# Another choice and order of seven-product pairs in the second feed-forward matrix of layer 1

## The chip, the cores and the metric

One NeuronCore of one Trainium2 chip runs the whole program. The times are device microseconds (us) of a run. In the profile PE is the matrix engine (PEld its weight loads), DVE the vector engine, ACT the scalar engine, POOL the general-purpose engine, and SP the queue that issues the loads from HBM. PSUM is the memory that matrix products accumulate in; it has eight banks here, each of 128 x 512 floats. SBUF is the memory that holds everything else.

## The reference

A two-layer decoder trunk for 256 tokens of width 2048, in float32. Layer 0 mixes tokens by retention, layer 1 by a short gated convolution; a SwiGLU feed-forward of width 5632 follows each, and a final RMSNorm closes the trunk. The change touches only the feed-forward of layer 1:

```
def swiglu(h, w_in, w_out):
    a, b = jnp.split(h @ w_in, 2, axis=-1)
    return (jax.nn.silu(a) * b) @ w_out
...
x = (x + g2 * swiglu(h, ffn_w_in[i], ffn_w_out[i])).astype(x.dtype)
```

`w_in` has 2048 x 11264 elements, `w_out` 5632 x 2048.

## The kernel before

**Products in three matmuls.** A float32 operand is written as hi + lo, two numbers that the matrix engine takes (`fp32r`). A product is then hi·hi + hi·lo + lo·hi, three matmuls (`triple`, lines 1190 to 1194: L1192, L1193, L1194). The weights come from HBM as float32, in loads of 128 x 2048 that `fetch` issues on SP (L388), three buffers in turn. `prepare` cuts a load into pieces of up to 1024 columns; for each, ACT makes hi (L426) and DVE makes lo = raw - hi (L429). There are four buffers for hi and four for lo, and `take` keeps up to three pieces ready.

**Pairs, plain and in sevens.** In layer 1's feed-forward (`swiglu_tokens`, `token_products`) the tokens are the rows of the result: two halves of 128 tokens by two column blocks of 512, which makes four results in four PSUM banks. The sum runs over *pairs* of 128-row weight tiles. One pair and four results are a 2 x 2 by 2 x 2 block product. A plain pair takes 8 block products, or 24 matmuls. A pair "in sevens" takes 7, or 21 matmuls, by a Strassen-Winograd scheme: three of them use blocks as they are, four use sums of blocks on both sides. Three of the seven go to the four result banks, four to four further banks:

```
plan = [
    ("m1", a11), (x_banks[1][0], s4), (x_banks[0][0], a12), ("m5", s1), ("m7", s3), ("m6", s2),
    (x_banks[0][1], a22),
]
```

The sums of the weight blocks are made for every load by DVE (L412, L417, L418); such a load is prepared in four pieces, of 512, 1024, 1024 and 1024 columns, and not in two of 1024. The sums of the other operand are made once per pair by `seven_sums` (L636 to L648): four DVE operations on 128 x 128 (L641 to L644), one ACT cast (L646), one DVE subtraction (L647). For pairs of the middle (silu(a) * b) they start from a float32 copy of the pair, made by ACT from PSUM (L1289) into a tile `full` that has one buffer. After the last pair in sevens of a group, ACT and DVE combine the four further banks (L1242 to L1246).

**Groups.** Each call of `token_products` is a group. I number them by matrix, part and place. The middle has 44 tiles, in two parts of 20 and 24 (`PART_TILES`):

- part 0: a first group in another form makes tiles 0 to 3, then *in 0.1* to *in 0.4* make 4 tiles (2 pairs) each; *out 0.0* and *out 0.1* multiply all 10 pairs with the second matrix, each for 1024 output columns.
- part 1: *in 1.0* to *in 1.5* make 12 pairs; *out 1.0* multiplies them for the first 1024 columns; the last 1024 columns are done in another form, with no sevens.

Every *in* group goes over 8 pairs of the input, with pairs 2, 4 and 6 in sevens: plain, plain, seven, plain, seven, plain, seven, plain. The *out* groups take their order from `ffn_token_groups` (L165 to L201). With the pairs of a part numbered from 0 and those in sevens in brackets, it is now 0 1 5 6 [2] 7 [3] [4] 8 9 in part 0 and 8 9 3 4 [0] 5 [1] 6 [2] 7 10 11 in part 1.

**Seams.** The tail of a group runs within the next one. `token_products` hands back "asides", which `ticked` starts after so many blocks of the next group's products. After an *in* group (`middle`, L1269) these are: the finals, silu and product for each token half during the next group's first pair, and, at the end of its second pair, `turned`: eight transposes on PE (L1264) into two PSUM banks, from which ACT and DVE make hi and lo of the new middle tiles (L1285, L1286) and, for a pair that will be taken in sevens, ACT makes `full`. After an *out* group (`outputs`, L1294) they are 16 transposes in two portions, and updates of the residual (L1303).

The eight PSUM banks are two lanes of four (L1187, L1203). A group's results use one lane, which changes from group to group; the further banks of its sevens use the other, and so do the transposes of the group before. The first pair in sevens of a group therefore takes its banks m1, m5, m7, m6 from those that the transposes have left.

**What sets the order.** PE's order is that of the program text (L290). DVE's and ACT's order in this stage is chosen by a planner from its own model of costs. SP issues loads in the order of use, each when one of the three `raw` buffers is free. The weights lie in HBM in the order of use (`in_use_order`, `laid_out`), so a new order of pairs makes another layout, and the same number of loads.

Of the kernel before, what the change touches and what calls it, by code (L numbers as in the profile page):

```python
# [50 lines left out]
TOKEN_LAYERS = (1,)  # L51
PART_TILES = (20, 24)
IN_SEVENS = {0: (), 1: (2, 4, 6)}
OUT_SEVENS = {0: 3, 1: 3}
RAW_BUFS = 3
PART_BUFS = 4
ROW_AT = 64
# [65 lines left out]
def led(cols):  # L123
    return [Group(cols[:LEAD])] + [Group([c]) for c in cols[LEAD:]]
# [35 lines left out]
def token_group(cols, pairs, sevens):  # L160

    return [Group.sevens(cols, p) if p in sevens else Group(cols, DV, p) for p in pairs]


def ffn_token_groups(layer):  # L165

    n = KT // 2
    rows = [(2 * i, 2 * i + 1) for i in range(n)]
    tiles = DV // P
    ins, outs, at = [], [], 0  # L170
    for part, size in enumerate(PART_TILES):
        groups = []
        for j in range(at // tiles, (at + size) // tiles):
            if j == 0:
                narrow = [q * DFF + i * P for i in range(tiles) for q in range(2)]
                groups += led(narrow)
            else:
                groups.append(token_group([j * DV, DFF + j * DV], rows, [rows[i] for i in IN_SEVENS[layer]]))
        ins.append(groups)
        pairs = [(at + 2 * i, at + 2 * i + 1) for i in range(size // 2)]  # L180
        fixed = pairs[:2] if part == 0 else pairs[-4:-2]
        late = pairs[-2:]
        rest = [p for p in pairs if p not in fixed + late]
        sevens = rest[: OUT_SEVENS[layer]]
        plain = rest[OUT_SEVENS[layer] :]
        mixed = fixed + plain[:2]
        plain = plain[2:]
        for p in sevens:
            mixed += [p] + plain[:1]
            plain = plain[1:]  # L190
        mixed += plain + late
        assert sorted(mixed) == pairs
        outs.append([])
        for half in range(2):
            c = half * 2 * DV
            if layer == DEPTH - 1 and part == 1 and half == 1:
                outs[-1].append([Group([c + i * P], ks=range(at, at + size)) for i in range(2 * tiles)])
            else:
                outs[-1].append(token_group([c, c + DV], mixed, sevens))
        at += size  # L200
    return ins, outs  # L201
# [7 lines left out]
FFN_IN = ffn_in_groups()  # L209
FFN_OUT = out_groups(halves(DFF), 2, LEAD_FFN)  # L210
FFN_TOKENS = {layer: ffn_token_groups(layer) for layer in TOKEN_LAYERS}


# [1217 lines left out]
```

## Time and profile before

| | us |
|---|---|
| runs | 2618.07, 2621.07, 2623.72; median 2621.07 |
| the profiled execution, as timed | 2622.86 |
| its span, first to last instruction | 2620.8 |
| PE busy | 2577.0 (98% of the span) |
| DVE busy | 2166.4 (83%) |
| ACT busy | 1296.0 (49%) |

In the views of the profile, a line such as L429 is a line of the kernel; `lo<-raw,hi` says which tile an operation writes and which it reads. Two rows of one engine overlap in time when the next instruction starts before the end of the last is over, so that distances between starts tell more of the rate than the lengths do. "Idle before" is how long the engine stood still, and the name behind the arrow is what ended that. A view of stretches gives, for each stretch of time, its length, the busy time of each engine and the clock that PE was granted, as a share of the full one.

### The profile page before, as it was taken

Reading aid. Unit: us, or ns where it says so; the run is one execution under the profiler, and the core shown is the slowest. Engines: PE = TensorE matmul, PEld = TensorE weight load, DVE = VectorE, ACT = ScalarE, POOL = GpSimd, SP = SyncE. Lnnn points to the kernel's source line nnn. Section 1 sums busy time; section 2 is a strip of 40 time slices with the busy share of each in tenths; the row PEclk is TensorE's granted clock in tenths of the full one; section 3 lists DMA queues with packets and bytes.
Section 4 is the critical chain, followed back from the end, with each engine's and each line's share of the span. In section 5 each row is a group of like instructions: output and inputs, shape, how many; then the busy total and the mean of one; then the engine's idle time right before and its main releaser. Section 6 shows DMA issues by size and latency. Waiting matters only on the chain.

```text
span 2620.8 us, 36671 instructions
## 1 busy us (share of the span) xinstructions
PE 2577.0 (98%) x14350; PEld 2244.8 (86%) x14350; DVE 2166.4 (83%) x2726; ACT 1296.0 (49%) x1747; POOL 128.5 (5%) x230
## 2 busy tenths in 40 slices
PE   6999999999999999999999999999999999999998
PEld 5998889888889888888888898888987888788887
DVE  7898878787698887777778889888888987898974
ACT  5544543444455544344444454444565544555553
POOL 0000000120000001100000100000000000000000
PEclk9999999999999999999999999999999999999999
DMA  9976668777686987878787768877755555455553
GB/s 399 395 276 239 230 229 319 275 291 275 242 303 238 339 321 292 299 297 300 289 302 286 299 230 327 322 289 284 262 187 183 193 205 181 177 193 203 200 192 129
DMA packets 96944, 687.48 MB, mean 262 GB/s; under 512 B 10753, under 2 KB 12545, under 8 KB 13825
## 3 DMA queue, kind: packets, MB, share of 16 engines
q1 hardware_dynamic: 96194, 684.48, 70.4%
q8 instruction: 112, 1.84, 0.3%
q10 hardware_dynamic: 576, 0.66, 0.1%
q14 instruction: 62, 0.51, 0.1%
HBM read 682.99 MB, written 2.10 MB: 261 GB/s over the span
## 4 chain that ended last, share of the span: by engine, by line
PE 67%; issue 28%; DVE 2%; DMA 1%; ACT 0%; POOL 0%; SPq 0%; POOLq 0%; ACTq 0%; DVEq 0%
PE bank L480 30%; PE bank L483 15%; PE bank L518 4%; PE bank L519 4%; PE bank L520 4%; PE bank L505 1%; PE bank L504 1%; PE bank L503 1%; PE bank L548 1%; PE bank L547 1%; PE bank L546 1%; PE bank L693 1%; PE bank L694 1%; PE bank L695 1%; DMA raw<-w_all 1%
## 5 line engine op out<-in xcount | busy, mean ns | idle before, releaser
L426 ACT CAST hi<-raw 128x1024 fp32r<-128x1024 f32 (+1 forms) x912 | 934.6, 1033 | 939.0 <-PE bank L480 357.0
L429 DVE TENSOR_TENSOR lo<-raw,hi 128x1024 fp32r<-128x1024 f32 (+1 forms) x912 | 1084.1, 1198 | 303.9 <-ACT hi L426 301.1
L480 PE MATMUL bank<-h,hi 128*128 128x512 f32 x2016 | 699.8, 392 | 0.0
L483 PE MATMUL bank<-h,lo 128*128 128x256 f32 x2016 | 565.6, 281 | 0.0
L480 PEld LDWEIGHTS bank<-h,hi 128*128 128x128 f32 x2016 | 377.8, 187 | 81.7
L483 PEld LDWEIGHTS bank<-h,lo 128*128 128x128 f32 x2016 | 381.8, 189 | 0.0
L332 DVE SCALAR_TENSOR_TENSOR raw<-raw,cb 128x2048 f32<-128x2048 f32 x160 | 365.6, 2285 | 17.2 <-DMA raw<-w_mod 17.1
L480 PE MATMUL bank<-mid,hi 128*128 128x512 f32 x922 | 320.1, 394 | 0.0
L483 PE MATMUL bank<-mid,lo 128*128 128x256 f32 x922 | 256.5, 278 | 0.4 <-DVE lo L429 0.4
L480 PEld LDWEIGHTS bank<-mid,hi 128*128 128x128 f32 x922 | 173.2, 188 | 39.5
L518 PE MATMUL bank<-hi,h 128*128 128x512 f32 x512 | 201.7, 394 | 0.0
L519 PE MATMUL bank<-lo,h 128*128 128x512 f32 x512 | 200.8, 392 | 0.0
L520 PE MATMUL bank<-hi,h 128*128 128x512 f32 x512 | 199.8, 390 | 0.0
L1192 PE MATMUL bank<-hi,h 128*128 128x512 f32 x490 | 193.3, 394 | 0.0
L1193 PE MATMUL bank<-lo,h 128*128 128x512 f32 x490 | 192.3, 392 | 0.0
L1194 PE MATMUL bank<-hi,h 128*128 128x512 f32 x490 | 192.1, 392 | 0.0
L483 PEld LDWEIGHTS bank<-mid,lo 128*128 128x128 f32 x922 | 173.4, 188 | 0.7 <-DVE lo L429 0.7
L480 PE MATMUL bank<-rm,hi 128*128 128x512 f32 x496 | 173.0, 395 | 0.0
L429 DVE TENSOR_TENSOR lo<-sums,hi 128x1024 fp32r<-128x1024 f32 x78 | 95.4, 1223 | 60.6 <-ACT hi L426 60.1
L426 ACT CAST hi<-sums 128x1024 fp32r<-128x1024 f32 x78 | 82.1, 1053 | 126.2 <-PE bank L1194 92.6
L483 PE MATMUL bank<-rm,lo 128*128 128x256 f32 x496 | 138.0, 278 | 0.0
L520 PEld LDWEIGHTS bank<-hi,h 128*128 128x128 f32 x512 | 96.6, 189 | 20.6
(230 smaller groups left out, 4095.6 us busy)
## 6 DMA issues: line engine op xcount, KB each, us to landing
raw<-w_all SPq DMA_DIRECT2D x456, 1024.0 KB, 4.9
raw<-w_mod SPq DMA_DIRECT2D x192, 1024.0 KB, 5.3
x<-x_in SPq DMA_DIRECT2D x4, 512.0 KB, 5.5
decay<-tab_in SPq DMA_DIRECT2D x8, 128.0 KB, 3.1
out<-x SPq DMA_DIRECT2D x4, 256.0 KB, 3.2
out<-x ACTq DMA_DIRECT2D x3, 128.0 KB, 2.6
out<-x SPq DMA_DIRECT2D x1, 384.0 KB, 2.6
out<-x ACTq DMA_DIRECT2D x1, 256.0 KB, 3.2
```

The costliest lines, as they stand in the source:

```text
L332: nc.vector.scalar_tensor_tensor(raw, raw, 1.0, cb, op0=ALU.mult, op1=ALU.mult, accum_out=total)
L426: nc.scalar.copy(hi[:, :n], raw)
L429: nc.vector.tensor_tensor(lo[:, :n], raw, hi[:, :n].bitcast(F32), op=ALU.subtract)
L480: nc.tensor.matmul(pt, hi, h, start=fresh and k == g.ks[0], stop=False, skip_group_check=True)
L483: nc.tensor.matmul(pt[:, 1, :], lo, h[:, 0, :], start=False, stop=last and k == g.ks[-1], skip_group_check=True)
L503: nc.tensor.matmul(pt, hi, h[:, 0, :], start=first, stop=False, skip_group_check=True)
L518: nc.tensor.matmul(flat(pt), a[:, 0, :], hi, start=first, stop=False)
L519: nc.tensor.matmul(flat(pt), a[:, 0, :], lo, start=False, stop=False)
L520: nc.tensor.matmul(flat(pt), a[:, 1, :], hi, start=False, stop=last)
L1192: nc.tensor.matmul(flat(pt), a[:, 0, :], hi, start=first, stop=False, skip_group_check=True)
L1193: nc.tensor.matmul(flat(pt), a[:, 0, :], lo, start=False, stop=False, skip_group_check=True)
L1194: nc.tensor.matmul(flat(pt), a[:, 1, :], hi, start=False, stop=last, skip_group_check=True)
```

## The change

In the *out* groups of layer 1 four pairs in place of three are taken in sevens, and every second pair of the part is chosen, beginning with pair 2 in part 0 and pair 0 in part 1. The first two places go to plain pairs, and then sevens and plain pairs alternate. The *in* groups, and the last 1024 columns of part 1, stay as they are.

```
-OUT_SEVENS = {0: 3, 1: 3}
+OUT_SEVENS = {0: 3, 1: 4}
...
         pairs = [(at + 2 * i, at + 2 * i + 1) for i in range(size // 2)]
-        fixed = pairs[:2] if part == 0 else pairs[-4:-2]
-        late = pairs[-2:]
-        rest = [p for p in pairs if p not in fixed + late]
-        sevens = rest[: OUT_SEVENS[layer]]
-        plain = rest[OUT_SEVENS[layer] :]
-        mixed = fixed + plain[:2]
-        plain = plain[2:]
-        for p in sevens:
-            mixed += [p] + plain[:1]
-            plain = plain[1:]
-        mixed += plain + late
+        sevens = pairs[2 - 2 * part :: 2][: OUT_SEVENS[layer]]
+        plain = [p for p in pairs if p not in sevens]
+        mixed = plain[:2]
+        for p, q in zip(sevens, plain[2:]):
+            mixed += [p, q]
+        mixed += plain[2 + len(sevens) :]
```

The order becomes 0 1 [2] 3 [4] 5 [6] 7 [8] 9 in part 0 and 1 3 [0] 5 [2] 7 [4] 8 [6] 9 10 11 in part 1. Since an *in* group makes two neighbouring pairs, no group makes two pairs in sevens any more: before, *in 0.1* made pairs 2 and 3 and *in 1.0* pairs 0 and 1, both of each in sevens, and *in 0.2* and *in 1.1* one each. Now *in 0.1* to *in 0.4* and *in 1.0* to *in 1.3* make one each. A fourth tile of sums (`msums3`) is held in SBUF.

## The prediction

> **What bounds the kernel now.** I read the page's busy times first, then who waited for whom in the last stage, then the groups of `token_products` as stretches of time.
>
> ```profile
> span 2620.8 us, 36671 instructions
> PE 2577.0 (98%) x14350; PEld 2244.8 (86%) x14350; DVE 2166.4 (83%) x2726; ACT 1296.0 (49%) x1747; POOL 128.5 (5%) x230
> ```
>
> PE is the bound: work taken from it shortens the run, and so does every wait of PE that goes. From 1850 us on, PE waited for this:
>
> ```profile
> PE bank L1192 <- ACT full L1289: 6.4, 2, 3.2
> PE bank L1193 <- DVE lo L429: 1.5, 2, 0.8
> ...
> PE bank L1192 <- ACT hi L426: 0.6, 2, 0.3
> ```
>
> Two waits of 3.2 us for the copy `full`, and four short ones for weight pieces. To place them I cut the stage at the first matmul of each group; the stretches are in 0.2, in 0.3, in 0.4, out 0.0, out 0.1, in 1.0, in 1.1, in 1.2, in 1.3, in 1.4, in 1.5, out 1.0.
>
> ```profile
> core 0: us, PE busy (x) PEld busy (x) DVE busy (x) ACT busy (x) POOL busy (x), PEclk, DMA share, GB/s
> 1967.60:2015.41 47.81, 44.57 (x193) 36.18 (x191) 41.19 (x54) 26.08 (x31) 0.00 (x0) 0.96 0.49 176
> 2015.41:2058.58 43.17, 43.12 (x192) 34.97 (x191) 38.66 (x48) 24.68 (x29) 0.00 (x0) 1.00 0.53 193
> 2058.58:2100.95 42.37, 42.37 (x192) 35.20 (x191) 39.06 (x45) 24.00 (x27) 0.00 (x0) 1.00 0.55 200
> 2100.95:2156.17 55.22, 54.14 (x241) 44.05 (x239) 44.33 (x50) 28.25 (x31) 0.00 (x0) 1.00 0.55 199
> 2156.17:2212.28 56.11, 55.04 (x249) 44.89 (x248) 44.04 (x52) 26.11 (x27) 0.00 (x0) 1.00 0.53 188
> 2212.28:2255.62 43.34, 43.34 (x200) 35.93 (x199) 37.99 (x46) 21.77 (x23) 0.00 (x0) 1.00 0.51 184
> 2255.62:2304.55 48.93, 45.66 (x193) 36.99 (x191) 41.20 (x54) 26.06 (x31) 0.00 (x0) 0.93 0.48 173
> 2304.55:2347.72 43.17, 43.12 (x192) 34.98 (x191) 38.70 (x48) 24.71 (x29) 0.00 (x0) 1.00 0.56 193
> 2347.72:2390.09 42.37, 42.37 (x192) 35.20 (x191) 39.12 (x45) 23.99 (x27) 0.00 (x0) 1.00 0.55 201
> 2390.09:2432.47 42.38, 42.38 (x193) 35.20 (x191) 38.30 (x44) 24.02 (x27) 0.00 (x0) 1.00 0.55 198
> 2432.47:2474.84 42.37, 42.37 (x192) 35.19 (x191) 38.30 (x44) 24.02 (x27) 0.00 (x0) 1.00 0.57 199
> 2474.84:2538.98 64.14, 64.14 (x289) 53.17 (x287) 49.26 (x54) 32.48 (x35) 0.00 (x0) 1.00 0.57 204
> ```
>
> The *in* groups all have the same products. Where the group before made no pair to be taken in sevens (in 1.3 to in 1.5, in 0.4) one lasts 42.37 us. Where it made one (in 0.3, in 1.2), 43.17. Where it made two (in 0.2, in 1.1), 47.81 and 48.93. So a seam with one such pair costs 0.80 us over 42.37, a seam with two 5.44 or 6.56.
>
> Why two are so dear shows in the order of time on ACT, and then on PE, in in 0.2:
>
> ```profile
> 1981.66 0.59 ACT L1289 COPY full<-bank 128x512 f32<-128x512 f32 x1
> ...
> 1985.33 0.62 ACT L646 CAST msums<-ssum 128x512 fp32r<-128x512 f32 x1 [1.37 <-DVE ssum L644]
> 1985.86 0.58 ACT L1289 COPY full<-bank 128x512 f32<-128x512 f32 x1
> 1986.49 0.60 PE L1192 MATMUL bank<-hi,rows 128*128 128x512 f32 x1 [3.23 <-ACT full L1289]
> 1986.89 0.63 PE L1193 MATMUL bank<-lo,rows 128*128 128x512 f32 x1
> ```
>
> `full` has one buffer, so the second copy, at 1985.86, comes after DVE has read the first (L644). Until then the transposes hold the second PSUM bank, and the first seven of the group waits for a bank. Behind the wait the matmuls start 0.40 us apart (1986.49, 1986.89), and the granted clock is 0.96 and 0.93 in these two groups, against 1.00: the stall is paid again as slow matmuls.
>
> **The change, part by part.** Next the time of a step: a seven and a plain pair undisturbed in in 1.5, and the third seven of out 0.0 and of out 0.1, which directly follows the second.
>
> ```profile
> 2454.44:2459.20 4.76, 4.76 (x22) 3.94 (x21) 3.69 (x5) 3.68 (x4) 0.00 (x0) 1.00 0.67 220
> 2459.20:2464.64 5.44, 5.44 (x25) 4.51 (x24) 5.37 (x7) 2.11 (x2) 0.00 (x0) 1.00 0.67 205
> 2138.57:2145.28 6.71, 5.63 (x22) 3.79 (x21) 5.54 (x7) 4.90 (x6) 0.00 (x0) 1.00 0.37 132
> 2194.68:2201.39 6.71, 5.64 (x22) 3.79 (x21) 5.54 (x7) 4.90 (x6) 0.00 (x0) 1.00 0.40 131
> ```
>
> *Removed matmuls.* A seven is 5.44 - 4.76 = 0.68 us shorter. Three more of them, one for each of out 0.0, out 0.1 and out 1.0: 2.04 us.
>
> *Removed: sevens in a row.* Two such steps, 6.71 - 4.76 = 1.95 each: 3.90 us. After the change a plain pair stands between any two. In the *in* groups and in out 1.0, which alternate already, nothing but the seam is lost: in 1.5 is 5 x 5.44 + 3 x 4.76 = 41.48 and 0.9 for the seam's transposes, and out 1.0 is 9 x 5.44 + 3 x 4.76 = 63.24 and the same 0.9. Out 0.0 and out 0.1 get the *in* groups' order, lengthened by one seven and one plain pair.
>
> *Moved: the sums.* Before, four seams carry them: in 0.2 and in 1.1 with two, in 0.3 and in 1.2 with one. Their excess over 42.37 is 5.44 + 6.56 + 0.80 + 0.80 = 13.60 us. After, eight seams have one each: in 0.2, 0.3, 0.4, out 0.0, in 1.1, 1.2, 1.3, 1.4. If x is the mean cost of such a seam, the whole change is
>
> 8x - 13.60 - 3.90 - 2.04 = 8x - 19.54 us.
>
> *What x is.* The nearest rows say 0.80, twice; there the group before had ended in step. With several such seams in a row that isn't so: in 0.4 and in 1.3 have no sums, yet DVE is busy for 39.06 and 39.12 us against 38.30 in in 1.4 and in 1.5. That is 0.76 to 0.82 us of work carried over from the seam group ahead. It is hidden there, as in 0.4 has slack; a next group with sums of its own may have none. So the two seams that begin a row (in 0.2, in 1.1) have x = 0.80, and the six that follow lie between 0.80 and 0.80 + 0.80 = 1.60. I take the middle, 1.20, since neither end has a row nearer to it: 2 x 0.80 + 6 x 1.20 = 8.8 us. The ends are 6.4 and 11.2. A result below 6.4 isn't excluded, as the order on DVE is chosen anew.
>
> *Added DVE and ACT work*, from the groups of instructions after 1850 us:
>
> ```profile
> L429 DVE TENSOR_TENSOR lo<-raw,hi 128x1024 fp32r<-128x1024 f32 x233 | 281.8, 1219 | 42.7 <-ACT hi L426 42.0
> L412 DVE TENSOR_TENSOR sums<-raw 128x1024 f32<-128x1024 f32 x39 | 47.5, 1218 | 0.0
> L418 DVE TENSOR_TENSOR sums<-raw,sums 128x512 f32<-128x512 f32 x39 | 26.9, 689 | 0.9
> L641 DVE TENSOR_TENSOR ssum<-full 128x128 f32<-128x128 f32 x9 | 2.5, 281 | 0.0
> L426 ACT CAST hi<-raw 128x1024 fp32r<-128x1024 f32 x232 | 241.6, 1053 | 159.2 <-PE bank L1194 110.4 <-PE bank L480 26.3 <-PE bank L694 5.7
> ```
>
> A plain load costs DVE 2 x 1.22 = 2.44 us. One in sevens costs three pieces of 1024 (3.66), L412 (1.22) and three operations on 512 columns (L417, L418, the first piece; 3 x 0.69): 6.95, so 4.51 more. The sums of a pair cost 4 x 0.28 + 0.69 = 1.81. A plain pair and a seven together need 9.39 of DVE in 5.44 + 4.76 = 10.20 of PE: DVE keeps up, barely, and that is why two in a row do not work. For out 0.0 I get 44.33 + 4.51 + 1.81 + 0.80 carried = 51.45 us of DVE in 6 x 5.44 + 4 x 4.76 + 0.9 + 1.2 = 53.8 us: 96%, against 92% in in 0.4, which runs undisturbed. Out 0.1 has 44.04 + 4.51 = 48.55 in 51.68 + 1.86 = 53.5 (1.86 is what in 1.0 has over 41.48, with the same kind of seam), and out 1.0 is loose. The PE time that hides this leaves 2.3 us in out 0.0; without it the addition would be on the path. ACT gets some 1.5 casts of 1.05 us more per seven, at 28.25 of 55.22 busy: hidden by its own idle time.
>
> *Nothing else.* As many loads are issued, in another order. The sums of pair 8 of part 0 arise in the first steps of out 0.0 and are read six steps later, some 30 us. Only pair 9 lies between the last seven of out 0.0 or out 0.1 and the next group, which needs the lane of the further banks; that is so in every *in* group, none of which starts late. The first seven now comes before the second portion of the residual's transposes, as in in 1.0 today, at no wait.
>
> **The sum:** 8.8 - 19.54 = -10.7 us. The profiled execution was timed at 2622.86, so 2612.1 by it. That is 1.8 over the median of the runs, 2621.07; against the median it is 2610.3.
>
> [...]
>
> **Rivals.**
>
> *The seams cost nothing.* If the planner finds room for one copy and one set of sums, x is 0 and the change is -19.5: 2601.5. Against it: both seams with one pair cost 0.80.
>
> *DVE becomes the bound in out 0.0.* When a seven is late, its last pieces come one after another:
>
> ```profile
> 2142.74 1.22 DVE L429 TENSOR_TENSOR lo<-sums,hi 128x1024 fp32r<-128x1024 f32 x1 [1.17 <-ACT hi L426]
> ```
>
> There DVE idles 1.17 us per seven for ACT's cast. Four of them make 51.45 + 4.68 = 56.1 against 53.8: +2.3, with x at 1.60 (11.2 - 19.54 = -8.3) together -6.0: 2615.1. For it: the 96%. Against it: in 0.4 by the same reckoning needs 39.06 + 3 x 1.17 = 42.6 of 42.37 and is undisturbed.
>
> *Only the matmuls are saved.* The planner may order ACT and DVE so that other waits, in these groups or in their neighbours, take the place of the old ones. Then the change gives its 2.04 us: 2619.0. For it: the order is not written by hand. Against it: ten groups alternate today without losing a step.
>
> *Slower: every seam waits.* If what holds the bank is not the second copy but any copy that comes while ACT and DVE are behind, a seam with one pair, behind another such seam, is as dear as in 0.2: x = 5.44, and 8 x 5.44 - 19.54 = +24.0: 2645. It gets slower than before from x = 19.54 / 8 = 2.44 us on. For it: the carried 0.8 us. Against it: the two seams with one pair, 0.80 each; no row shows such a seam behind another.
>
> **Chances.** The forecast, -8.3 to -13.1 (2608.0 to 2612.8): 0.70. Seams free, 2601.5: 0.06. DVE bound, 2615.1: 0.08. Only the matmuls, 2619.0: 0.10. Slower: 0.06. The measurement tells no change from one under 0.2%, 5.2 us, that is 2615.8 here. Faster is the first two and half of the third, 0.80; same is the other half and the fourth, 0.14; slower 0.06. The range leaves out half of "seams free", "only the matmuls" and "slower", 0.19: from 2603 to 2616.5.
>
> **What would show it.** The wait of PE for ACT full L1289 goes from 6.4 us to under 1, with eight copies in place of six. In 0.2 and in 1.1 last about 43.2 us at clock 1.00; in 0.4, in 1.3 and in 1.4 grow to 43.2 to 44.0; out 0.0 is near 53.8, out 0.1 near 53.5, out 1.0 near 63.5. No seven of the *out* groups but a first lasts over 5.0 us. I am wrong if the seams grow beyond 1.6, if PE waits for DVE lo in out 0.0, or if the groups behave so and the run is not faster.

## The result, and the profile after

The changed kernel takes 2609.98 us (median of 5 runs, 2606.47 to 2615.93) against 2621.16 us before (median of 5). The ratio is 0.9958, with a 95% interval of 0.9943 to 0.9974: faster by 0.26 to 0.57%. The profiled execution was timed at 2609.98 us, 12.9 us under that of before. Line numbers after L201 are smaller by 5 now: L1192 has become L1187, L429 L424, L1289 L1284, the lines of `seven_sums` L636 to L642.

From the page after, the span and the busy times:

```profile
span 2608.2 us, 36705 instructions
PE 2573.7 (99%) x14341; PEld 2239.0 (86%) x14341; DVE 2178.9 (84%) x2751; ACT 1299.5 (50%) x1757; POOL 130.7 (5%) x230
```

PE has 9 matmuls and as many weight loads less (14341 for 14350), DVE 12.5 us more work. What PE waited for from 1850 us on, in the changed kernel:

```profile
PE bank L1188 <- DVE lo L424: 2.3, 6, 0.4
...
```

The two waits of 3.2 us for the copy `full` are gone, and so is the wait for ACT hi. Six short waits for DVE, at most 0.4 us long, have come in their place. The three left out, of 0.7 to 1.0 us, stand in the kernel before too. The groups after, as stretches cut in the same way, from in 0.2 to out 1.0; the last row is the whole stage, from the start of in 0.1 to the end of out 1.0:

```profile
core 0: us, PE busy (x) PEld busy (x) DVE busy (x) ACT busy (x) POOL busy (x), PEclk, DMA share, GB/s
1966.83:2010.01 43.18, 43.16 (x193) 34.95 (x191) 38.70 (x48) 24.71 (x29) 0.00 (x0) 1.00 0.55 194
2010.01:2053.34 43.33, 42.94 (x192) 35.00 (x191) 39.42 (x49) 24.60 (x29) 0.00 (x0) 1.00 0.54 195
2053.34:2096.66 43.32, 42.93 (x192) 35.00 (x191) 39.41 (x49) 24.60 (x29) 0.00 (x0) 1.00 0.54 194
2096.66:2149.95 53.29, 52.91 (x237) 43.53 (x236) 48.74 (x59) 30.26 (x35) 0.00 (x0) 1.00 0.56 199
2149.95:2203.51 53.56, 53.56 (x246) 44.34 (x244) 48.04 (x57) 27.57 (x29) 0.00 (x0) 1.00 0.54 197
2203.51:2246.85 43.34, 43.34 (x200) 35.90 (x199) 39.03 (x48) 21.77 (x23) 0.00 (x0) 1.00 0.55 194
2246.85:2290.01 43.16, 43.11 (x192) 34.94 (x191) 38.68 (x48) 24.68 (x29) 0.00 (x0) 1.00 0.55 193
2290.01:2333.39 43.38, 43.00 (x193) 35.01 (x191) 39.47 (x49) 24.61 (x29) 0.00 (x0) 1.00 0.56 195
2333.39:2376.71 43.32, 42.99 (x192) 35.01 (x191) 39.41 (x49) 24.60 (x29) 0.00 (x0) 1.00 0.54 194
2376.71:2420.03 43.32, 42.93 (x193) 35.00 (x191) 39.42 (x49) 24.62 (x29) 0.00 (x0) 1.00 0.55 194
2420.03:2462.40 42.37, 42.37 (x192) 35.17 (x191) 39.06 (x45) 24.00 (x27) 0.00 (x0) 1.00 0.58 202
2462.40:2525.86 63.46, 63.46 (x286) 52.59 (x285) 53.14 (x59) 34.02 (x37) 0.00 (x0) 1.00 0.58 206
1925.31:2525.86 600.55, 598.23 (x2677) 490.79 (x2676) 536.56 (x635) 332.61 (x379) 0.00 (x0) 1.00 0.55 197
```

The stage before, in the same cut:

```profile
1926.07:2538.98 612.91, 604.14 (x2686) 496.33 (x2684) 524.17 (x610) 328.72 (x369) 0.00 (x0) 0.99 0.54 193
```

So 12.36 us of the 12.6 by which the span got shorter lie in this stage. The dear seams are gone (in 0.2 47.81 to 43.18, in 1.1 48.93 to 43.16) and the clock is 1.00 in every group. The length of this stage varies little from one execution to another: the changed kernel, profiled again in a later run, shows 600.71. The time ahead of it varies more, by 2.5 us among most of the profiles here. I therefore read the experiments by the stage first, and by the timed ratio second.

### The profile page after: what moved, and what is told of

It reads as the page before. It is cut to its first block, busy times and chain, and to the rows that moved or that the text cites. A ratio compares the mean times of both kernels' runs of the same rounds, so it can differ in the third digit from the quotient of the medians.

```text
span 2608.2 us, 36705 instructions
## 1 busy us (share of the span) xinstructions
PE 2573.7 (99%) x14341; PEld 2239.0 (86%) x14341; DVE 2178.9 (84%) x2751; ACT 1299.5 (50%) x1757; POOL 130.7 (5%) x230
## 4 chain that ended last, share of the span: by engine, by line
PE 67%; issue 28%; DVE 2%; DMA 2%; ACT 0%; POOL 0%; SPq 0%; POOLq 0%; ACTq 0%; DVEq 0%
PE bank L475 30%; PE bank L478 15%; PE bank L513 4%; PE bank L514 4%; PE bank L515 4%; PE bank L500 1%; PE bank L499 1%; PE bank L498 1%; DMA raw<-w_all 1%; PE bank L543 1%; PE bank L542 1%; PE bank L541 1%; PE bank L688 1%; PE bank L689 1%; PE bank L690 1%
## 5 line engine op out<-in xcount | busy, mean ns | idle before, releaser
L424 DVE TENSOR_TENSOR lo<-raw,hi 128x1024 fp32r<-128x1024 f32 (+1 forms) x912 | 1081.6, 1196 | 292.2 <-ACT hi L421 287.9
L1187 PE MATMUL bank<-hi,h 128*128 128x512 f32 x490 | 191.7, 391 | 0.0
L421 ACT CAST hi<-sums 128x1024 fp32r<-128x1024 f32 x84 | 88.5, 1054 | 128.3 <-PE bank L1189 78.1
L424 DVE TENSOR_TENSOR lo<-sums,hi 128x1024 fp32r<-128x1024 f32 x84 | 102.7, 1223 | 50.4 <-ACT hi L421 49.4
```

Source lines behind the costliest of these rows:

```text
L421: nc.scalar.copy(hi[:, :n], raw)
L424: nc.vector.tensor_tensor(lo[:, :n], raw, hi[:, :n].bitcast(F32), op=ALU.subtract)
L1187: nc.tensor.matmul(flat(pt), a[:, 0, :], hi, start=first, stop=False, skip_group_check=True)
```

## Experiments

**Alternation alone.** The kernel before, with its own pairs, in an order that puts a plain pair between any two:

```
-        mixed = fixed + plain[:2]
...
+        order = (0, 1, 5, 6, 2, 7, 3, 8, 4, 9) if part == 0 else (8, 9, 3, 4, 0, 5, 1, 6, 2, 7, 10, 11)
+        mixed = [pairs[i] for i in order]
```

> The kernel before, with its own pairs in sevens (2, 3, 4 and 0, 1, 2), but a plain pair between any two: 0 1 5 6 [2] 7 [3] 8 [4] 9 in part 0; part 1 alternates already. Theory (the terms add): only the two steps of 6.71 us go, 3.9 us, so about 2617.2; in 0.2 and in 1.1 still take 47.8 and 48.9 us. Rival (the order makes the whole gain, the choice of pairs none): 12 us, about 2609, and the dear seams go too.

Measured: 2619.55 us, ratio 0.9990 (0.9981 to 1.0000). In 0.2, out 0.0 and the whole stage:

```profile
1968.11:2015.95 47.84, 44.60 (x193) 36.16 (x191) 41.20 (x54) 26.07 (x31) 0.00 (x0) 0.96 0.49 176
2101.47:2154.73 53.26, 53.26 (x241) 44.20 (x239) 43.20 (x48) 28.26 (x31) 0.00 (x0) 1.00 0.56 199
...
1926.59:2535.74 609.15, 602.53 (x2686) 496.51 (x2685) 523.87 (x610) 328.71 (x369) 0.00 (x0) 0.99 0.54 194
```

The stage is 3.76 us shorter, as the theory has it (3.9). Out 0.0 falls from 55.22 to 53.26, and in 0.2 stays dear. The order alone isn't the gain. The timed difference, 1.5 us, is itself near what can be told; its interval (0 to 5 us) holds the 3.8.

**Spread alone.** Three sevens, two of them in a row as before, but every second pair:

```
+        sevens = pairs[2 - 2 * part :: 2][: OUT_SEVENS[layer]]
+        order = (0, 1, 3, 5, 2, 7, 4, 6, 8, 9) if part == 0 else (8, 9, 1, 3, 0, 5, 2, 6, 4, 7, 10, 11)
+        mixed = [pairs[i] for i in order]
```

Part 0 is then 0 1 3 5 [2] 7 [4] [6] 8 9. Out 1.0 alternates, as before.

> Three sevens as before, two of them in a row in each out group as before, but every second pair: 0 1 3 5 [2] 7 [4] [6] 8 9 and 8 9 1 3 [0] 5 [2] [6 plain] [4] 7 10 11, so no group makes two. Theory: the seams cost 0.80 + 0.95 + 0.95 in each part, 5.4 us in place of 13.6, so 8.2 us less, about 2612.9; in 0.2 and in 1.1 last 43.2; the third seven of out 0.0 and out 0.1 still takes 6.7. Rival (the order makes the gain): no change, 2621.

Measured: 2614.88 us, ratio 0.9971 (0.9960 to 0.9981). In 0.2, out 0.0, the stage:

```profile
1968.55:2011.69 43.14, 43.12 (x193) 34.95 (x191) 38.66 (x48) 24.68 (x29) 0.00 (x0) 1.00 0.53 193
2098.38:2153.59 55.21, 54.12 (x240) 44.03 (x239) 45.07 (x51) 28.34 (x31) 0.00 (x0) 1.00 0.55 200
...
1927.03:2531.76 604.73, 600.95 (x2685) 492.62 (x2684) 522.71 (x610) 327.05 (x369) 0.00 (x0) 1.00 0.55 195
```

The stage is 8.18 us shorter, the 8.2 of the theory. The dear seams go by the choice of pairs, while out 0.0 keeps the 55.21 of two sevens in a row. The two parts together are 3.76 + 8.18 = 11.94.

**Three sevens in the new order.**

```
-OUT_SEVENS = {0: 3, 1: 4}
+OUT_SEVENS = {0: 3, 1: 3}
```

> The changed kernel with three sevens in place of four in the out groups (pairs 2, 4, 6 and 0, 2, 4). Theory: it loses 3 x 0.68 = 2.0 us of matmuls and gains the two seams that the fourth pairs of sums cost, 0.72 and 0.94 us, so it is 0.4 us slower than the changed kernel, not to be told from it by the time; out 0.0 and in 1.4 then last 48.6 + 5.4 and 42.4 us. Rival (the fourth seven is worth its matmuls): 2.0 us slower, with the seams unchanged elsewhere.

Measured: 2612.12 us, ratio 0.9961 (0.9946 to 0.9976). Out 0.0, in 1.4, the stage:

```profile
2096.13:2149.39 53.26, 53.26 (x241) 44.18 (x239) 46.19 (x52) 28.22 (x31) 0.00 (x0) 1.00 0.60 208
2376.77:2419.14 42.37, 42.37 (x193) 35.19 (x191) 39.05 (x45) 24.00 (x27) 0.00 (x0) 1.00 0.60 201
1924.82:2525.65 600.83, 599.21 (x2685) 492.84 (x2684) 522.43 (x610) 326.80 (x369) 0.00 (x0) 1.00 0.56 196
```

12.08 us under the kernel before: the two parts add up (11.94). Against the changed kernel the stage is longer by 0.28 us only (by 0.12 against the later profile). The fourth pair in sevens is worth nearly nothing: its 2.0 us of matmuls are paid back at the two more seams that carry sums. By the rows, these cost 0.71 us in out 0.0 and 0.95 in in 1.4 of the changed kernel, and nothing here. (The expectation's length of out 0.0, 54.0, was reckoned wrongly; 7 x 5.44 + 3 x 4.76 + 0.9 is 53.26.)

**Two buffers for the copy.** The kernel before, with `bufs=2` for the tile `full` in both places:

```
-                    full = fpool.tile([P, 2, S], F32, tag="full", name=name("full"), bufs=1)
+                    full = fpool.tile([P, 2, S], F32, tag="full", name=name("full"), bufs=2)
```

> The kernel before with two buffers for the copy full in place of one, nothing else. Theory (the second copy waits for the one buffer, and holds the bank): the waits of PE for ACT full fall from 6.4 us to under 1; in 0.2 and in 1.1 fall to between 43.2 and 45.0 us (two pairs of sums still cost DVE 1.8 us more than one), the whole to between 2610.8 and 2614.3. Rival (two pairs of sums are too much work for DVE, whatever the buffer): no change.

Measured: 2613.69 us, ratio 0.9968 (0.9955 to 0.9980). Two of PE's waits in the stage, then in 0.2 and the stage:

```profile
PE bank L1193 <- DVE lo L429: 1.5, 2, 0.8
PE bank L1192 <- ACT full L1289: 0.9, 2, 0.5
```

```profile
1968.69:2012.17 43.48, 42.99 (x192) 35.03 (x191) 40.67 (x54) 25.89 (x31) 0.00 (x0) 1.00 0.55 191
1927.17:2531.35 604.18, 600.30 (x2685) 492.88 (x2684) 523.19 (x610) 328.35 (x369) 0.00 (x0) 1.00 0.55 195
```

The wait for the copy falls from 6.4 to 0.9 us, and in 0.2 from 47.81 to 43.48. That is the cause the prediction gave: the second copy waited for its one buffer, and held a bank. DVE had the same sums to make. One more buffer in the kernel before gets 8.7 of the 12.4 us without any new order.

**Two pairs of one group again.** The changed kernel, four sevens that alternate, but two each from a group:

```
-        sevens = pairs[2 - 2 * part :: 2][: OUT_SEVENS[layer]]
+        sevens = [pairs[2 - 2 * part + i] for i in (0, 1, 4, 5)]
```

> The changed kernel, four sevens, none next to another, but two of them from one group: pairs 2, 3, 6, 7 and 0, 1, 4, 5. Theory (a group that makes two pairs in sevens costs 5.4 to 6.6 us at its seam, one with none nothing): four such seams, in 0.2, 0.4, 1.1, 1.3, about 24 us in place of 7.1, so 17 us slower than the changed kernel, about 2627, slower than the kernel before. Rival (it is the number of pairs that counts, not their place): 2610, as the changed kernel.

Measured: 2628.86 us, ratio 1.0016 (1.0007 to 1.0025), slower than the kernel before. The four dear seams, in 0.2, in 0.4, in 1.1 and in 1.3:

```profile
1968.79:2016.40 47.61, 44.37 (x192) 36.05 (x191) 41.20 (x54) 26.08 (x31) 0.00 (x0) 0.96 0.49 177
2058.78:2105.00 46.22, 42.94 (x192) 35.02 (x191) 41.10 (x54) 26.18 (x31) 0.00 (x0) 1.00 0.52 182
2254.45:2302.31 47.86, 44.59 (x193) 36.15 (x191) 41.20 (x54) 26.07 (x31) 0.00 (x0) 0.96 0.50 175
2344.68:2393.70 49.02, 45.75 (x192) 37.10 (x191) 41.20 (x54) 26.07 (x31) 0.00 (x0) 0.93 0.48 171
```

The one wait of PE in these groups:

```profile
PE bank L1187 <- ACT full L1284: 12.9, 4, 3.2
```

The seams cost 5.24, 3.85, 5.49 and 6.65 us over 42.37, 21.2 in all; the theory had about 24. By the stage the run is 14.1 us longer than the changed kernel (614.64 for 600.55), by the medians 17.4 longer than the changed kernel measured again below (2611.45); the theory had 17. The timed runs spread from 2623.65 to 2630.51 us, the longer ones with a lower mean clock (0.993 for 0.994 to 0.996), and the profiled one, 2625.82, is among the shorter. It is the place of the pairs that counts, not their number.

**Sums on POOL.** POOL is idle in this stage (0.00 us busy in every row of it above). The changed kernel with the four sums of a pair on POOL, then with the last subtraction there too:

```
-        nc.vector.tensor_tensor(s1, a21, a22, op=ALU.add)
+        nc.gpsimd.tensor_tensor(s1, a21, a22, op=ALU.add)
...
-        nc.vector.tensor_tensor(dst[:, 1], s, dst[:, 0].bitcast(F32), op=ALU.subtract)
+        nc.gpsimd.tensor_tensor(dst[:, 1], s, dst[:, 0].bitcast(F32), op=ALU.subtract)
```

> The changed kernel with the four sums of each pair (L636 to L639) on POOL in place of DVE; the last subtraction stays on DVE. Theory (what is left of a seam, 0.94 us, is DVE work that comes when DVE is late): 4 x 0.2 us of DVE less per seam, so the seams behind a seam fall from 43.3 us to between 42.6 and 43.0, 3 to 5 us less in all, 2605 to 2607. Rival (the bank held by the copy is what a seam costs): no change, 2610. POOL needs about 0.7 us for one such operation by the nearest row (128 x 256), which is late only if the sums are then missing at the out group.

> As the run with the four sums on POOL, and the last subtraction (L642) on POOL too. Theory (DVE's work at the seam): another 0.6 us of DVE gone, the seams behind a seam come near the 42.4 of a group without sums, 42.4 to 42.7, some 5 to 7 us less than the changed kernel, 2603 to 2605. Rival (the bank): 2610.

Measured: 2625.18 us (ratio 1.0006, 0.9997 to 1.0016) and 2621.95 us (0.9999, 0.9990 to 1.0008). Both expectations fell: the whole gain is gone. In order of time, POOL and then DVE behind the transposes in in 0.2 of the first, and ACT in the second:

```profile
1989.35 1.35 POOL L636 TENSOR_TENSOR ssum<-full 128x128 f32<-128x128 f32 x1 [72.72 <-ACT full L1284]
1990.66 1.44 POOL L638 TENSOR_TENSOR ssum<-full 128x128 f32<-128x128 f32 x1
1992.07 0.46 POOL L637 TENSOR_TENSOR ssum<-ssum,full 128x128 f32<-128x128 f32 x1
```

```profile
1989.17 2.62 DVE L424 TENSOR_TENSOR lo<-raw,hi 128x1024 fp32r<-128x1024 f32 x2
1993.76 0.69 DVE L642 TENSOR_TENSOR msums<-ssum,msums 128x512 fp32r<-128x512 f32 x1 [1.97 <-ACT msums L641]
```

```profile
1989.95 0.62 ACT L641 CAST msums<-ssum 128x512 fp32r<-128x512 f32 x1 [2.88 <-POOL ssum L639]
```

POOL needs 1.35 and 1.44 us for the first two sums and 0.46 or 0.47 for the other two; DVE takes 0.28 for each. So a slower engine need not be the whole of it: the two long sums run beside subtractions of DVE, and the two short ones while DVE stands idle. The two subtractions take 2.62 us here, and two in a row at 2001.99 in the same view take 2.35. What made both longer side by side, no run here tries by itself.

The chain of copy, sums, cast and subtraction gets longer, and the members on ACT and DVE stand ahead of the weights' casts and subtractions in their queues. Those wait with them: from 1900 to 2540 us DVE lo stands 61.1 and 73.0 us for ACT hi, against 56.0 in the changed kernel profiled beside them. So in 0.2 takes 44.46 and 44.07 us in place of 43.18:

```profile
1974.62:2019.08 44.46, 43.32 (x193) 34.94 (x192) 38.55 (x45) 24.54 (x29) 3.64 (x4) 1.00 0.53 187
```

```profile
1971.47:2015.54 44.07, 43.25 (x192) 34.94 (x191) 39.33 (x44) 24.68 (x29) 4.86 (x5) 1.00 0.53 190
```

The whole stage is longer by 9.0 and 6.4 us (609.72 and 607.15 us, against 600.71 in the changed kernel profiled beside them); the spans are longer by 14.9 and 9.4 (2624.7 and 2619.2, against 2609.8). The rest lies ahead of the stage: it starts at 1933.1 and 1930.0 in place of 1927.3, and in the group ahead of in 0.1, where the input's three pairs get their sums, PE has a wait that the kernel before has not:

```profile
PE bank L466 <- DVE low L705: 2.4, 1, 2.4
```

With the last subtraction on POOL too, this wait is 3.5 us. That it is the same chain there I have not shown.

**The changed kernel again**, beside these on one chip:

> The changed kernel itself, beside the two with POOL on the same chip. Every theory: as before, 2610, in 0.2 at 43.2 and the followers at 43.3 us.

Measured: 2611.45 us, ratio 0.9951 (0.9938 to 0.9964), the stage 600.71 us. So POOL's loss is no matter of the chip.

**The sums later.** If the sums cost because they stand in ACT's and DVE's queues just where these are late, they should be put elsewhere. The changed kernel, with `seven_sums` in an aside of its own, 76 or 46 blocks behind the transposes; the copy `full` stays:

```
-                    sums_of[n] = seven_sums(full, f"msums{list(sums_of).index(n)}")
+                    held[n] = full
...
+        def sums():
+            for n, full in held.items():
+                sums_of[n] = seven_sums(full, f"msums{list(sums_of).index(n)}")
...
+        later = [(46, sums)] if at in sums_of or at + 2 in sums_of else []
+        return [(8, lambda: product_of(0)), (8, lambda: product_of(1)), (16, turned)] + later
```

> The changed kernel with the sums of a pair (L636 to L642) taken out of the transposes' aside into one of their own, 76 blocks later, in the last plain pair of the group (of the same group, in out 0.0 just ahead of pair 8). The copy full stays where it is. Theory (the sums cost because DVE and ACT are already late right behind the transposes; later the next two plain pairs give the time back): seams fall from 43.3 to between 42.4 and 42.7 us, the whole 4 to 7 us less than the changed kernel, 2603 to 2606; in out 0.0 the sums may be late by up to 2 us. Rival (DVE has the same work in all, so the time only moves): within 1.5 us of 2610.

> The same with the sums 46 blocks behind the transposes, in the middle of the alternating pairs. Theory (DVE keeps up with a plain pair and a seven with 0.4 us or so to spare, so 1.4 us more in the middle of them is paid in part): seams between 42.4 and 43.0, 2604 to 2608, and out 0.0 is not late. Rival: 2610.

Measured: 2606.63 us (ratio 0.9940, 0.9926 to 0.9954) with 76 and 2605.57 us (0.9936, 0.9923 to 0.9948) with 46. With 46: in 0.2, in 0.3, out 0.0 and the stage:

```profile
1967.18:2009.90 42.72, 42.70 (x192) 35.12 (x191) 39.25 (x49) 24.81 (x29) 0.00 (x0) 1.00 0.55 196
2009.90:2052.62 42.72, 42.67 (x192) 35.12 (x191) 39.35 (x49) 24.89 (x29) 0.00 (x0) 1.00 0.55 197
2095.36:2148.28 52.92, 52.87 (x237) 43.57 (x236) 48.44 (x58) 30.60 (x35) 0.00 (x0) 1.00 0.55 199
1925.66:2521.92 596.26, 595.89 (x2676) 491.89 (x2675) 536.15 (x635) 334.67 (x379) 0.00 (x0) 1.00 0.56 198
```

A seam now costs 42.72 - 42.37 = 0.35 us, behind another seam as well. DVE has the same work in the stage (536.15 against 536.56 us), and not one wait for DVE is left in it. So what a seam costs beyond 0.35 us is a matter of when the sums are made, not of how much DVE has to do. With both delays the stage is 4.3 us shorter than the changed kernel's. With 46 the seams and the time are as expected; with 76 the time is 0.6 us over the expected 2603 to 2606. This is the fastest version here. Between 46 and 76 the measurement can't tell.

## Why the prediction was right

**The two terms that carry it** were sized as measured. Sevens in a row: 3.90 us predicted, 3.76 by the order alone. Their cause (too little time for DVE) was not tried by itself; shown is that a plain pair between them takes the cost away. The dear seams: the formula 8x - 19.54 stands, with the cause shown by the second buffer and by the two-of-a-group run.

**x was sized too high.** I took 0.80 for the two seams that begin a row and 1.20 for the six that follow. By the stretches after, over 42.37, they are 0.81, 0.96, 0.95 in part 0, and 0.79, 1.01, 0.95, 0.95 in part 1; out 0.0, whose steps and transposes make 51.68 + 0.9, has 0.71. The sum is 7.1 and not 8.8, so the change is -12.4 and not -10.7 in the stage. Between the ends that I set (0.80 and 1.60) the truth lay near the lower: the carried work is there, since in 1.5 still has 39.06 us of DVE, but PE pays only a part of it. The fourth seven's own step turned out as 2.04 - 1.66 (out 0.0 and in 1.4, 0.71 + 0.95) = 0.4 us, 0.28 measured.

**The forecast of the total** was 2610.3, and the median is 2609.98. It is partly luck: the stage got 12.4 us shorter where the sum had 10.7, but the medians only 11.2 us, since the profiled execution of before lay 1.8 us over its median, as I had taken into account, and that of after lay on it. For the profiled execution the forecast was 2612.1, 2.1 us too long.

**The rivals.** "Seams free" is wrong in the changed kernel, 7.1 us in place of none, though it is nearly what the sums put later reach. "DVE becomes the bound in out 0.0" is wrong: DVE is busy 48.74 of 53.29 us, 91%, not the 96% that I reckoned. The step at fault there is in the main the addition of DVE lengths: rows of one engine overlap, and out 0.0 gained 4.4 us of DVE with a seven and a pair's sums, for which I had 4.51 + 1.81 + 0.80 = 7.1. The lengths of the rows that start in the group add up to 47.5 us before and 53.6 after, 6.2 more, so overlap accounts for 1.8 of the 2.7 us; where the other 0.9 went is not shown. "Only the matmuls" is wrong by the same rows. "Every seam waits" is wrong: with eight copies no wait of PE for ACT full is left, by the waits shown first. The view of the copy's line in the changed kernel:

```profile
L1284 ACT COPY full<-bank x8: 587/595/596, 1980.9 to 2390.1; 128x512 f32<-128x512 f32 x8
```

The late piece is a new, small one instead: in the groups behind a seam, the second seven waits up to 0.4 us for DVE lo.

**What was to show it** held, but for two: I said that no seven of the *out* groups but a first lasts over 5.0 us, and that I am wrong if PE waits for DVE lo in out 0.0. The second seven of out 0.0 is one of those that wait, 0.4 us for DVE lo, and lasts 5.42 us. That sign of being wrong came true, then, but small: out 0.0 is 0.71 us over its steps, and DVE does not bound it. Here is the DVE piece that comes before in the same place of in 0.3:

```profile
2031.88 1.22 DVE L424 TENSOR_TENSOR lo<-sums,hi 128x1024 fp32r<-128x1024 f32 x1
2033.02 0.69 DVE L413 TENSOR_TENSOR sums<-raw,sums 128x512 f32<-128x512 f32 x1
2034.90 1.23 DVE L424 TENSOR_TENSOR lo<-sums,hi 128x1024 fp32r<-128x1024 f32 x1 [1.20 <-ACT hi L421]
```

The last sum of the weights (L413) was put behind the subtraction for the first sums; ACT can cast only then, and DVE stands 1.20 us. I had this row's like in the rival of the late seven, at the right place and with too high a price.

**The clock.** The four waits of the two-of-a-group run have one length (12.9 us in all, the longest 3.2), yet in 0.2, in 1.1 and in 1.3 show a granted clock of 0.96, 0.96 and 0.93, and in 0.4 shows 1.00. So the wait's length alone does not decide here. The steps of the clock in the trace say more: it falls from 1.00 to 0.50 at 1987.22, 2273.94 and 2362.68 us, which lie 286.72 and 88.74 us apart (84 and 26 times 3.413), and stays there for 3.41, 3.41 and 6.83 us. This is the run cut on that grid, two stretches each around the waits of in 0.2 and of in 0.4, and the two slow ones of in 1.3:

```profile
1983.81:1987.22 3.41, 0.65 (x3) 0.19 (x1) 3.41 (x8) 1.89 (x4) 0.00 (x0) 1.00 0.01 2
1987.22:1990.63 3.41, 2.95 (x7) 2.37 (x8) 3.41 (x8) 0.41 (x1) 0.00 (x0) 0.50 0.94 308
2072.56:2075.97 3.41, 1.83 (x7) 0.86 (x5) 3.41 (x7) 2.43 (x4) 0.00 (x0) 1.00 0.00 0
2075.97:2079.38 3.41, 1.71 (x7) 1.42 (x8) 3.41 (x7) 1.12 (x3) 0.00 (x0) 1.00 0.57 163
...
2362.68:2366.09 3.41, 2.52 (x6) 2.06 (x7) 3.41 (x8) 0.84 (x2) 0.00 (x0) 0.50 0.77 276
2366.09:2369.51 3.42, 3.42 (x9) 2.68 (x9) 2.47 (x4) 1.56 (x2) 0.00 (x0) 0.50 0.09 36
```

In in 0.2 most of the wait lies in one stretch, in which PE is busy for 0.65 of 3.41 us, and the next stretch is slow. In in 1.1 and in 1.3 the stretch ahead of the step has 0.59 and 1.03 us of PE. In in 0.4 the wait is split over two stretches with 1.83 and 1.71 us of PE, and neither is followed by a slow one. Behind the waits PE runs at half the clock for 2.95, 3.41 and 5.94 us; half of that, 1.5, 1.7 and 3.0 us, is near what the groups take over in 0.4 (1.4, 1.6 and 2.8). How little PE work in a stretch brings the clock down, these few waits don't show. The kernel before shows steps of the same kind. This is its trace cut around the waits of in 0.2 and of in 1.1:

```profile
1983.33:1986.74 3.41, 0.25 (x1) 0.25 (x2) 3.41 (x8) 1.72 (x3) 0.00 (x0) 1.00 0.18 34
1986.74:1990.15 3.41, 3.41 (x9) 2.63 (x9) 2.91 (x8) 0.89 (x1) 0.00 (x0) 0.50 0.66 276
2270.05:2273.46 3.41, 1.19 (x4) 0.49 (x3) 3.41 (x8) 1.89 (x4) 0.00 (x0) 1.00 0.03 5
2273.46:2276.87 3.41, 2.36 (x6) 1.88 (x7) 3.41 (x8) 1.00 (x2) 0.00 (x0) 0.50 0.83 259
2276.87:2280.29 3.42, 3.42 (x10) 2.65 (x9) 2.54 (x5) 1.56 (x2) 0.00 (x0) 0.50 0.12 48
```

The two falls, at 1986.74 and 2273.46, are 286.72 us apart here too, and the stretches ahead of them have 0.25 and 1.19 us of PE work. Behind the first, matmuls start 0.43 us apart (1987.31, 1987.74), and 0.23 once the clock is 1.00 again (1990.24, 1990.47).

## What to carry to other kernels

Before an extra buffer or a new order is weighed, find what a stalled engine's *releaser* is waiting for: here a copy out of PSUM waited for an SBUF buffer, and so a bank was held; one buffer more, or one such pair per group, repairs it about equally (8.7 and 8.2 us of the stage). Work that is small in sum can be dear by its place in an engine's order: the same sums cost 0.9 us behind the transposes and 0.35 us some steps later, and a move to an idle engine, on which they took longer (0.46 to 1.44 us each for 0.28), made the stage 9.0 and 6.4 us longer, since their followers stayed in the busy queues. And a saving in matmuls has to be set against what feeds it: the fourth pair in sevens took away 2.0 us of PE and gave 1.7 back.

## What the runs showed of the hardware that I had not expected

A wait of PE of nearly one length was paid very differently. In the four dear seams of the two-of-a-group run, whose groups hold the same work, the group's excess is 3.85 us at a granted clock of 1.00, 5.24 and 5.49 at 0.96, and 6.65 at 0.93. The clock was at 0.50 for none, one or two stretches of 3.41 us, and that came to up to 2.8 us. A stretch with 0.59 to 1.03 us of PE work came ahead of each fall (0.25 and 1.19 in the kernel before); where the wait was split into stretches with 1.83 and 1.71 us, none came.

POOL took 1.35 and 1.44 us for the first two sums (128 x 128, both inputs in SBUF) beside subtractions of DVE, and 0.46 for the next with DVE idle. DVE takes 0.28.
